# Hybrid decoder layer on one core: the up projection's issue order written by hand, its sums put back into PSUM, and some low parts moved from GpSimd to VectorE

## The chip, the cores and the metric

The kernel runs on one core of one Trainium2 chip. The metric is the device time of one execution in microseconds (us), the median of several runs. Engines are named as in the profile: PE is TensorE (its matmuls), PEld its weight loads, DVE VectorE, ACT ScalarE, POOL GpSimd, SP SyncE, which issues most DMAs here. A name such as L1346 is a line of the kernel before; lines of the changed kernel are given as such.

## What is computed

One decoder layer over 1024 tokens of 1024 channels: an attention mixer and a state-space mixer side by side, merged through `w_o`, normalised, and then a gated MLP with a causal depthwise convolution of width 3:

```python
mix = (sigmoid(g_a) * y_a + sigmoid(g_b) * y_b) @ w_o
x = layer_norm(alpha * x + gate1 * mix) * ln1_g + ln1_b

h2 = layer_norm(x) * (1.0 + scale2) + shift2
up = causal_depthwise_conv(h2 @ w_up, conv_w, conv_b)     # 1024 -> 2 * 2816
val, gte = split(up, 2, axis=-1)
ff = (silu(gte) * val) @ w_down                            # 2816 -> 1024
x = layer_norm(alpha * x + gate2 * ff) * ln2_g + ln2_b
```

The change touches the stretch from the rows of `w_o` to the end of the up projection, `h2 @ w_up` with convolution and gate.

## The kernel before

**Precision.** A float32 operand is split into a high part (copied by ACT into a narrower format, fp32r) and a low part (value minus high part). A product takes three matmuls: high by high, high by low, low by high (L1346 to L1348).

**Rows of `w_o`** (L1403 to L1442). Eight rows of 128 tokens. Each is 48 matmuls on PE, then a residual sum `hr` on DVE (L1420), two layer norms (DVE statistics, ACT scaling), and the store of `x1`. Rows 0 to 5 apply the first norm's gain on DVE and its bias on POOL (L1425, L1426), rows 6 and 7 with two DVE instructions (`ln_affine`). The rows are then transposed by PE in `h2_rows`, first rows 0 to 3 together, then 4 and 5, then 6 and 7. The first half of the output tiles is scaled by DVE (L1213), the second by ACT (L1215). Results are `y0` (tokens 0 to 511) and `y1` (512 to 1023).

**Up projection.** The output is worked through in 22 pairs `f`, each 128 value channels and the 128 gate channels that go with them. Instead of eight block products of half the inner dimension and half the tokens, a pair takes seven products (Strassen's scheme), numbered 1 to 7. Product `j` multiplies a combination of weight blocks, made anew for each pair, with a combination of `h2` blocks `ops[j]`, made once (3, 5, 6, 7 lie in tiles `h2a`, 1, 2, 4 in `h2b`). Each is 12 matmuls of 128x512 (4 inner chunks by 3). Products gather in four PSUM banks: `Z` (2, then 4 on top) and `Y` (5, then 3 on top) are the two halves of one two-bank tile `up`; `X` (1, then 7) and `V` (6) are tiles of their own (`upX`, `upV`). Tile's dependency tracking treats the two halves of `up` as one tile.

- Weight combinations of a pair: `plain` (products 2 and 5: ACT copy L1295, low part on POOL L1296), `less` (3 and 4: DVE subtractions L1306, ACT copy L1309, low part on DVE L1310), `cross` (1: DVE L1314, ACT L1315, POOL L1316), `sums` (6 and 7: DVE L1321, ACT L1322, POOL L1323).
- Sums between products: `t` takes a copy of product 2 by ACT (L1357), then adds product 5 on DVE (L1355); `r` is product 1 minus `t` on DVE (L1359). `t` and `r` are SBUF tiles that a profile names `bias` (in one pair `upt`).
- `finish` makes the four quarters of the pair: `Y` and `Z` are complete in PSUM, the other two are added up by DVE in an SBUF tile `u` (L1368 to L1371). Then comes the convolution for the gate (`e` = 1) and the value (`e` = 0): tap 0 on ACT (L1379), taps 1 and 2 on DVE (L1382), two narrow DVE instructions across the seam of the token halves (L1384), Silu on ACT (L1386), the product of gate and value on POOL (L1387) and the store of `ff_d`.

**Operands.** `set_operand` makes a part of `ops[j]`: the sum on one engine (L1196), the high part on ACT (L1198), the low part on `e1` (L1199). In `h2_sums` `e1` is DVE or POOL in turn.

**Order.** The whole program goes through Tile's scheduler, which simulates it and puts every engine's instructions in an order of its own choosing; the order of the code above is only a start. In the steady part PE's order in a step is 2, 6 and 5 of the pair, 1 of the next pair, then 4, 3 and 7. Engines execute in order; an instruction that waits holds up all behind it on its engine. The down projection (L1561 to L1574) follows; its first matmuls (`dn`) need low parts of `w_down` and of `ff`.

Of the kernel before, what the change touches and what calls it, by code (L numbers as in the profile page):

```python
# [33 lines left out]
def kernel(  # L34
# [1166 lines left out]
    def h2_rows(i0, ni, ys):  # L1201
        n = P * ni
        for q in range(4):
            p = ps(name="h2p")
            if ni == 4:
                p1 = ps(name="h2p")
            for e in range(2):
                k = q + 4 * e
                pe = (p, p1)[e] if ni == 4 else p[:, n * e:n * e + n]
                for i4 in range(ni):  # L1210
                    TE.transpose(pe[:, P * i4:P * i4 + P], h2s[i0 + i4][:, P * k:P * k + P], ident)
                if e == 0:
                    V.tensor_scalar(ys[q][e], pe, mod[:, 2, k:k + 1], mod[:, 3, k:k + 1], op0=OP.mult, op1=OP.add)  # L1213
                else:
                    A.activation(ys[q][e], pe, AF.Identity, bias=mod[:, 3, k:k + 1], scale=mod[:, 2, k:k + 1])  # L1215
# [63 lines left out]

    class Pair:  # L1280
        def __init__(self, f):
            self.f, self.w, self.bank, self.done, self.t = f, {}, {}, set(), None
# [5 lines left out]
        def plain(self, es):  # L1288
# [4 lines left out]
            for e in es:  # L1293
                src = self.c1[:, 4:8] if e else self.c0[:, 0:4]
                A.activation(h[:, e], src, AF.Copy)  # L1295
                G.tensor_sub(l[:, e], src, h[:, e].bitcast(F32))  # L1296
                w[5 if e else 2] = h[:, e], l[:, e]

        def less(self, es):
            w = self.w  # L1300
            if 0 in es:
                self.t34 = wtile("C", "uh"), wtile("C", "ul"), Bt([P, 2, 4, P], name="us")
            h, l, t = self.t34
            for e in es:
# [1 line left out]
                V.tensor_sub(t[:, e], src[:, 4 * e:4 * e + 4], src[:, 4 - 4 * e:8 - 4 * e])  # L1306
# [3 lines left out]
            V.tensor_sub(l[:, v], t[:, v], h[:, v].bitcast(F32))  # L1310

        def cross(self):
            t, t1 = wtile("C", "u1"), Bt([P, 4, P], name="us1")
            V.tensor_add(t1, self.c0[:, 0:4], self.c1[:, 4:8])  # L1314
            A.activation(t[:, 0], t1, AF.Copy)  # L1315
            G.tensor_sub(t[:, 1], t1, t[:, 0].bitcast(F32))  # L1316
            self.w[1] = t[:, 0], t[:, 1]

        def sums(self):
            h, l, t = wtile("wh", "uh"), wtile("wl", "ul"), Bt([P, 2, 4, P], name="us")  # L1320
            V.tensor_add(t.rearrange("p a k c -> p (a k) c"), self.c0, self.c1)  # L1321
# [1 line left out]
            G.tensor_sub(l, t, h.bitcast(F32))  # L1323
# [10 lines left out]
        def product(self, j, part=None):  # L1334
# [9 lines left out]
            for q in range(4):  # L1344
# [3 lines left out]
                TE.matmul(po, wl[:, q], h, start=False, stop=(q == 3), skip_group_check=True)  # L1348

            t, r = self.parts()  # L1350
            if j in (2, 5):
                if j == 2 and 5 in self.done:
                    V.tensor_add(t[:, c], po, t[:, c])
                elif j == 5 and 2 in self.done:
                    V.tensor_add(t, po, t)  # L1355
                else:
                    A.activation(t[:, c], po, AF.Copy)  # L1357
            elif j == 1:
                V.tensor_sub(r, po, t)  # L1359
            self.done.add(j)  # L1360

        def finish(self):
            bk = self.bank
            t, r = self.parts()
            lo, hi = slice(0, 512), slice(512, 1024)
            u = Bt([P, 1024], name="u")
            ug, uv = u[:, lo], u[:, hi]
            V.tensor_add(ug, bk["V"], r)  # L1368
            V.tensor_add(ug, ug, bk["Y"])  # L1369
            V.tensor_sub(uv, bk["X"], t)  # L1370
            V.tensor_add(uv, uv, bk["Z"])  # L1371
            cv = [Bt([P, 1024], name="cv") for _ in range(2)]

            for e, (a, b) in ((1, (bk["Y"], ug)), (0, (uv, bk["Z"]))):
                m = self.f + NF * e
                dst = cv[e]
                tap = lambda d: cw[:, 2 - d, m:m + 1]
                for half, src in ((lo, a), (hi, b)):
                    A.activation(dst[:, half], src, AF.Identity, bias=cw[:, 3, m:m + 1], scale=tap(0))  # L1379
                for d in (1, 2):  # L1380
                    for c0, src, n in ((d, a, 512 - d), (512 + d, b, 512 - d)):
                        V.scalar_tensor_tensor(dst[:, c0:c0 + n], src[:, 0:n], tap(d), dst[:, c0:c0 + n],  # L1382
                                               op0=OP.mult, op1=OP.add)
                    V.scalar_tensor_tensor(dst[:, 512:512 + d], a[:, 512 - d:512], tap(d), dst[:, 512:512 + d],  # L1384
                                           op0=OP.mult, op1=OP.add)
# [219 lines left out]
```

## Time and profile before

| | us |
|---|---|
| runs before | 1692.97, 1693.41, 1701.58 (median 1693.41) |
| the profiled execution | 1698.03 |
| its span, first to last instruction | 1696.3 |
| PE busy in the span | 1569.0 (92%) |
| DVE busy | 1239.6 (73%) |
| ACT busy | 691.1 (41%) |
| POOL busy | 706.2 (42%) |

Stages are cut by what PE works on: the rows of `w_o` end at 920 us, the up projection's first products and its fill-up run from there to about 1035 us, the steady pairs from 1035.3 to 1381.2 us, then come two last pairs and the down projection to the end. A timeline row gives start, duration, engine, line, operation, output<-inputs, and in brackets how long the engine was idle before it and on whom it waited. A group row gives the count, the summed and the mean time in ns. Matmuls overlap: what counts is the distance between two starts.

### The profile page before, as it was taken

How to read it: one execution, taken by the hardware profiler on the slowest of the kernel's cores; microseconds unless marked ns; L12 is line 12 of the kernel's file. 1: busy time of each engine (PE TensorE's matmuls, PEld its weight loads, DVE VectorE, ACT ScalarE, POOL GpSimd, SP SyncE). 2: the span in 40 equal slices, each digit the busy share in tenths (PEclk: the TensorE clock that was granted, in tenths of full speed). 3: DMA queues.
4: the chain of work that ended last, by engine and by line, in shares of the span. 5: the costliest groups of instructions: out<-in, count | busy, mean ns of one | idle time of the engine just before them, and what ended most of it. 6: DMA issues, size and time to landing. Idle time of an engine off the chain costs nothing.

```text
span 1696.3 us, 21512 instructions
## 1 busy us (share of the span) xinstructions
PE 1569.0 (92%) x7707; PEld 1304.0 (77%) x7707; DVE 1239.6 (73%) x2263; ACT 691.1 (41%) x1303; POOL 706.2 (42%) x584
## 2 busy tenths in 40 slices
PE   6987899999999999999998579999999998899996
PEld 4976787878989999788787357777777776688885
DVE  8699766565399999553658876888888888855448
ACT  4423223224399999421323433444344333311101
POOL 4342355400066566222536634544444555521105
PEclk8998999999999999999999789999999999999998
DMA  9235544622200010443411112222222227522102
GB/s 341 70 113 151 167 146 152 202 64 79 71 20 1 14 38 2 145 132 123 137 62 63 38 50 87 75 75 75 75 75 75 75 88 251 208 100 99 39 2 99
DMA packets 150128, 164.36 MB, mean 97 GB/s; under 512 B 20633, under 2 KB 123777, under 8 KB 150021
## 3 DMA queue, kind: packets, MB, share of 16 engines
q1 hardware_dynamic: 146357, 151.74, 27.9%
q10 hardware_dynamic: 3664, 11.24, 1.7%
q8 instruction: 61, 1.00, 0.2%
q14 instruction: 46, 0.38, 0.1%
HBM read 132.04 MB, written 30.91 MB: 96 GB/s over the span
## 4 chain that ended last, share of the span: by engine, by line
PE 57%; DVE 27%; issue 6%; ACT 5%; POOL 2%; DMA 2%; SPq 0%; DVEq 0%; ACTq 0%; POOLq 0%
DVE cv L1382 5%; PE dn L1472 4%; PE dn L1474 4%; PE dn L1473 4%; PE oacc L1008 3%; PE pT L1019 3%; PE up L1346 3%; PE up L1348 2%; PE up L1347 2%; DVE us L1321 2%; PE zm L128 2%; PE zm L130 2%; ACT cv L1379 2%; PE zm L129 2%; DVE us L1306 2%
## 5 line engine op out<-in xcount | busy, mean ns | idle before, releaser
L982 POOL TENSOR_SCALAR Pm<-Pm,gate,fc 128x64 f32<-128x64 f32 (+4 forms) x192 | 123.8, 659 | 57.3 <-DVE fc L980 56.8
L1472 PE MATMUL dn<-dnh,fh 128*128 128x512 f32 x320 | 124.9, 390 | 4.5 <-DVE facc L1570 4.5
L1296 POOL TENSOR_TENSOR ul<-wr,uh 128x512 fp32r<-128x512 f32 x44 | 77.7, 1785 | 115.4 <-ACT uh L1295 115.4
L1474 PE MATMUL dn<-dnh,fl 128*128 128x512 f32 x320 | 124.1, 389 | 1.6 <-DVE fl L1463 1.6
L1570 DVE SCALAR_TENSOR_TENSOR facc<-facc,dn 128x512 f32<-128x512 f32 x96 | 64.7, 681 | 83.3 <-PE dn L1474 83.3
L1473 PE MATMUL dn<-dnl,fh 128*128 128x512 f32 x320 | 124.5, 389 | 0.0
L978 ACT ACTIVATE Pm<-Pm,ng 128x64 f32<-128x64 f32 (+6 forms) x192 | 114.7, 602 | 6.5 <-DVE ng L959 5.0
L130 PE MATMUL zm<-hTh,wl 128*128 128x512 f32 x256 | 101.8, 398 | 13.1 <-DVE wl L113 13.1
L112 ACT ACTIVATE wh<-wr 128x1024 fp32r<-128x1024 f32 (+3 forms) x59 | 57.7, 978 | 137.8 <-PE ya L129 30.6
L111 POOL TENSOR_TENSOR wr<-wr,g2b 128x1024 f32<-128x1024 f32 x22 | 63.3, 2885 | 120.5 <-DMA wr<-in_w_down_dram 79.4
L1023 DVE TENSOR_TENSOR Pt<-pT,Pt 128x512 fp32r<-128x512 f32 (+1 forms) x160 | 100.6, 642 | 9.7 <-ACT Pt L1022 8.7
L128 PE MATMUL zm<-hTh,wh 128*128 128x512 f32 x256 | 101.9, 398 | 2.9 <-ACT wh L112 2.5
L1008 PE MATMUL oacc<-Pt,Vs 128*128 128x256 f32 x528 | 102.6, 304 | 0.9 <-DVE Pt L1023 0.4
L129 PE MATMUL zm<-hTl,wh 128*128 128x512 f32 x256 | 101.2, 395 | 0.0
L113 DVE TENSOR_TENSOR wl<-wr,wh 128x1024 fp32r<-128x1024 f32 (+2 forms) x40 | 51.8, 1294 | 64.4 <-ACT wh L112 64.2
L1019 PE MATMUL pT<-ident,Pm 128*128 128x128 f32 x592 | 91.3, 273 | 1.9 <-DVE yl L1082 1.0
L1379 ACT ACTIVATE cv<-u,cw 128x512 f32<-128x512 f32 x44 | 35.6, 809 | 140.3 <-DVE u L1369 132.7
L1022 ACT ACTIVATE Pt<-pT 128x512 fp32r<-128x512 f32 (+1 forms) x160 | 87.4, 560 | 13.1 <-PE pT L1019 12.1
L1382 DVE SCALAR_TENSOR_TENSOR cv<-u,cw,cv 128x511 f32<-128x511 f32 x88 | 74.8, 851 | 19.7 <-ACT cv L1379 18.8
L1347 PE MATMUL up<-h2b,uh 128*128 128x512 f32 (+1 forms) x184 | 72.2, 393 | 15.1 <-POOL h2b L1199 15.1
L1346 PE MATMUL up<-h2b,uh 128*128 128x512 f32 (+1 forms) x184 | 74.4, 406 | 12.1 <-DVE bias L1355 9.0
L1323 POOL TENSOR_TENSOR ul<-us,uh 128x1024 fp32r<-128x1024 f32 x22 | 52.8, 2398 | 74.8 <-ACT uh L1322 71.2
(507 smaller groups left out, 4871.0 us busy)
## 6 DMA issues: line engine op xcount, KB each, us to landing
wr<-in_w_up_dram SPq DMA_DIRECT2D x44, 512.0 KB, 3.8
wr<-in_w_in_dram SPq DMA_DIRECT2D x32, 512.0 KB, 4.2
wr<-in_w_ada_dram SPq DMA_DIRECT2D x32, 512.0 KB, 4.1
ff_d<-cv SPq DMA_DIRECT2D x22, 512.0 KB, 2.8
wr<-in_w_down_dram SPq DMA_DIRECT2D x22, 512.0 KB, 4.0
fl<-ff_d SPq DMA_DIRECT2D x22, 512.0 KB, 6.0
ar<-in_w_ada_dram SPq DMA_DIRECT2D x16, 512.0 KB, 9.4
zm_d<-sg ACTq DMA_DIRECT2D x16, 512.0 KB, 2.9
```

Of the source, the lines that this page charges most:

```text
L128: TE.matmul(po, wh, rh, start=start, stop=False, skip_group_check=skip)
L129: TE.matmul(po, wh, rl, start=False, stop=False, skip_group_check=skip)
L130: TE.matmul(po, wl, rh, start=False, stop=stop, skip_group_check=skip)
L978: A.activation(Pm[ii][:, c0:c0 + n], Pm[ii][:, c0:c0 + n], AF.Exp, bias=ng[:, ii, br:br + 1], scale=-1.0, accum_out=dn[:, ii, br:br + 1])
L982: G.tensor_scalar(Pm[ii][:, c0:c0 + n], Pm[ii][:, c0:c0 + n], gate[:, i, 3 * h + br:3 * h + br + 1], fc[:, ii, br:br + 1], op0=OP.mult, op ...
L1008: TE.matmul(acc[:, a0:a0 + 256], vt, ptile[:, hl, 256 * w:256 * w + 256], start=(first and n == 1), stop=(last and n == nmm), skip_group_c ...
L1019: TE.transpose(p[:, o:o + P], Pm[e][:, c0:c0 + P], ident)
L1346: TE.matmul(po, wh[:, q], h, start=(q == 0 and j not in (3, 4, 7)), stop=False, skip_group_check=True)
L1382: V.scalar_tensor_tensor(dst[:, c0:c0 + n], src[:, 0:n], tap(d), dst[:, c0:c0 + n], op0=OP.mult, op1=OP.add)
L1472: TE.matmul(p, ff[0][:, c0], wd[0][:, s], start=(e == 0), stop=False)
L1473: TE.matmul(p, ff[0][:, c0], wd[1][:, s], start=False, stop=False)
L1474: TE.matmul(p, ff[1][:, c0], wd[0][:, s], start=False, stop=(e == len(fs) - 1))
```

## The change

- `h2_rows`: all scaling of transposed tiles is done by ACT. `h2_sums`: all low parts are done by DVE. All eight rows use `ln_affine`. `h2_first` is called after row 4 instead of 5, `h2_next(0)` after row 6 instead of after the rows.
- `Pair`: the low parts of `plain`, `cross` and `sums` go to DVE for pairs 0 and 1 (`self.e`), to POOL for the others. The methods are cut into an add, a high and a low step, so that they can be put at different places. `less`'s low tile moves to another SBUF pool.
- `finish` becomes `value_hi`, `value_lo`, `gate_sum`, `gate` and `out`. The tile `u` is gone: the value's first half is added up in bank `X`, the gate's second half in bank `V`, both by DVE instructions that write PSUM, and ACT and DVE take all taps from PSUM.
- The reading of products 1, 2 and 5 becomes `take(j)`, which in pairs from 2 on is called where the step puts it.
- Pairs 1 to 21 run in `step(f)`, inside `tc.manual_schedule`, which keeps DVE, ACT, POOL and PE in the order of the code. PE's order is 2, 5, 1, 4, 7, 6, 3. What follows the last pair (loading `g2b`, which scales `w_down`, then `ff` and `x1`) now stands behind the loop.

```diff
@@ h2_rows
-                if e == 0:
-                    V.tensor_scalar(ys[q][e], pe, mod[:, 2, k:k + 1], mod[:, 3, k:k + 1], op0=OP.mult, op1=OP.add)
-                else:
-                    A.activation(ys[q][e], pe, AF.Identity, bias=mod[:, 3, k:k + 1], scale=mod[:, 2, k:k + 1])
+                A.activation(ys[q][e], pe, AF.Identity, bias=mod[:, 3, k:k + 1], scale=mod[:, 2, k:k + 1])
@@ h2_sums
-            e0, e1 = (V, (V if q % 2 else G)) if c1 - c0 < 512 else (V, (V if q else G))
-            set_operand(j, q, a, b, op, e0, e1, c0, c1, a if j != 2 else None)
+            set_operand(j, q, a, b, op, V, V, c0, c1, a if j != 2 else None)
@@ class Pair
+            self.e = V if f < 2 else G
...
-                G.tensor_sub(l[:, e], src, h[:, e].bitcast(F32))
+                self.e.tensor_sub(l[:, e], src, f32(h[:, e]))
...
+        def take(self, j, c=slice(0, 512)):
             t, r = self.parts()
+            po = self.bank["Z" if j == 2 else "Y" if j == 5 else "X"][:, c]
+            if j == 1:
                 V.tensor_sub(r, po, t)
+            elif 7 - j in self.done:
+                V.tensor_add(t[:, c], po, t[:, c])
+            else:
+                A.activation(t[:, c], po, AF.Copy)
...
+        def value_hi(self):
+            t, _ = self.parts()
+            Z = self.bank["Z"]
+            self.tap0(0, hi, Z)
+            V.tensor_sub(t, Z, t)
+            self.taps(0, hi, Z)
+        def value_lo(self):
+            t, _ = self.parts()
+            X = self.bank["X"]
+            V.tensor_add(X, X, t)
+            self.tap0(0, lo, X)
+            self.taps(0, lo, X)
+            self.seam(0, X)
+        def gate_sum(self):
+            _, r = self.parts()
+            V.tensor_add(r, self.bank["V"], r)
+        def gate(self):
+            _, r = self.parts()
+            Y, g = self.bank["Y"], self.bank["V"]
+            V.tensor_add(g, Y, r)
+            self.tap0(1, lo, Y)
+            self.tap0(1, hi, g)
+            self.taps(1, lo, Y)
+            self.taps(1, hi, g)
+            self.seam(1, Y)
@@ rows of w_o
-        hr = (Ct if i < 4 else Bt)([P, 1024], name="hr")
+        hr = (Ct if i < 6 else Bt)([P, 1024], name="hr")
-        if i >= 6:
-            ln_affine(xi, hr, l1g, l1b)
-        else:
-            normalize(xi, hr)
-            V.tensor_mul(xi, xi, l1g)
-            G.tensor_add(xi, xi, l1b)
+        ln_affine(xi, hr, l1g, l1b)
@@ the loop over pairs
+    def step(f):
+        pr, last = pairs[f], pairs.pop(f - 1)
...
+        two = product(2)
+        last.gate()
+        if two:
+            pr.take(2)
+        last.out()
+        five = product(5)
+        if nx:
+            nx.cross_add()
+            nx.less_sub((0, 1))
+            nx.cross_hl()
+            nx.less_hi((0, 1))
+        if five:
+            pr.take(5)
+        if nx:
+            nx.plain((1, 0))
+            nx.sums_add()
+        product(1)
+        if f > 1:
+            pr.take(1)
+        if nx:
+            nx.less_lo((0, 1))
+        product(4)
+        pr.value_hi()
+        product(7)
+        pr.value_lo()
+        product(6)
+        pr.gate_sum()
+        if nx:
+            nx.sums_hl()
+        product(3)
+    with tc.manual_schedule(engines={V.engine, A.engine, G.engine, TE.engine}):
+        for f in range(1, NF):
+            step(f)
```

**VectorE in a steady step.** Of the kernel before, from the first gate sum on (`u` is the SBUF tile, `bias` is `t` or `r`, `wr` the raw weights, `us` their combinations):

```order
L1368 TENSOR_TENSOR u<-upV,bias 128x512
L1369 TENSOR_TENSOR u<-u,up 128x512
L1382 SCALAR_TENSOR_TENSOR cv<-u,cw,cv 128x511
L1382 SCALAR_TENSOR_TENSOR cv<-u,cw,cv 128x510
L1370 TENSOR_TENSOR u<-upX,bias 128x512
L1371 TENSOR_TENSOR u<-u,up 128x512
L1314 TENSOR_TENSOR us_10416<-wr 128x512
L1306 TENSOR_TENSOR us<-wr 128x512 x2
L1321 TENSOR_TENSOR us<-wr 128x1024
```

Of the changed kernel, from the gate's sum of the pair before on:

```order
L1431 TENSOR_TENSOR upV<-up,bias 128x512
L1400 SCALAR_TENSOR_TENSOR cv<-up,cw,cv 128x511
L1400 SCALAR_TENSOR_TENSOR cv<-up,cw,cv 128x510
L1400 SCALAR_TENSOR_TENSOR cv<-upV,cw,cv 128x511
L1400 SCALAR_TENSOR_TENSOR cv<-upV,cw,cv 128x510
L1406 SCALAR_TENSOR_TENSOR cv<-up,cw,cv 128x1
L1406 SCALAR_TENSOR_TENSOR cv<-up,cw,cv 128x2
L1333 TENSOR_TENSOR us_10033<-wr 128x512
L1311 TENSOR_TENSOR us<-wr 128x512 x2
L1387 TENSOR_TENSOR bias<-up,bias 128x512
L1344 TENSOR_TENSOR us<-wr 128x1024
L1385 TENSOR_TENSOR bias<-upX,bias 128x512
```

The gate's taps now come all at once and read PSUM; the weight combinations follow in one piece with the take of product 5 (L1387) in between, the wide one (L1344) behind it, and then the take of product 1 (L1385).

**ScalarE in a steady step.** Before, the copy of product 2 (L1357) with what stands around it:

```order
L1379 ACTIVATE cv<-up,cw 128x512
L1379 ACTIVATE cv<-u,cw 128x512
L1357 ACTIVATE bias<-up 128x512
L1315 ACTIVATE u_10271<-us_10272 128x512
L1309 ACTIVATE uh<-us 128x1024
```

In the changed kernel the copy is L1389, behind the gate's two first taps (L1395) and ahead of Silu (L1440):

```order
L1395 ACTIVATE cv<-up,cw 128x512
L1395 ACTIVATE cv<-upV,cw 128x512
L1389 ACTIVATE bias<-up 128x512
L1440 ACTIVATE cv<-cv 128x1024
L1337 ACTIVATE u_10183<-us_10176 128x512
L1315 ACTIVATE uh<-us 128x1024
```

On PE product 5, which follows product 2 directly now, writes the other half of the tile that this copy reads; before, product 6 stood between them.

**GpSimd from the last operand in `h2a` to the steady part.** Before (`h2b`, `h2a` are low parts of operands, `ul` and `u_...` those of weights):

```order
L1199 TENSOR_TENSOR h2a<-h2s,h2a 128x512
L1296 TENSOR_TENSOR ul<-wr,uh 128x512
L1199 TENSOR_TENSOR h2b<-bias,h2b 128x256 x2
L1199 TENSOR_TENSOR h2b<-h2y,h2b 128x256 x3
L1199 TENSOR_TENSOR h2b<-bias,h2b 128x256
L1199 TENSOR_TENSOR h2b<-h2y,h2b 128x256
L1199 TENSOR_TENSOR h2a<-h2y,h2a 128x512 x2
L1199 TENSOR_TENSOR h2b<-bias,h2b 128x256
```

In the changed kernel, where L1441 is the product of gate and value of pair 0:

```order
L1199 TENSOR_TENSOR h2a<-h2y,h2a 128x512 x4
L1441 TENSOR_TENSOR cv<-cv 128x1024
L1338 TENSOR_TENSOR u_9064<-us_9057,u_9064 128x512
L1302 TENSOR_TENSOR ul<-wr,uh 128x512 x2
L1350 TENSOR_TENSOR ul<-us,uh 128x1024
```

All that stood between them on POOL (the low parts of operands 1, 2, 4, 6, 7 and of the weights of pairs 0 and 1) stands in VectorE's queue now.

More of the change, by code (lines that the diff above doesn't have):

```diff
@@ L1312, in cross @@
[L1312 to L1316, printed above, removed]
[L1317 to L1321 removed]
+            A.activation(self.t34[0][:, v], self.us[:, v], AF.Copy)
@@ new lines, in less_lo, with less, cross_add @@
+        def less_lo(self, es):
+            h, l = self.t34
+            v = slice(None) if len(es) == 2 else es[0]
+            V.tensor_sub(l[:, v], self.us[:, v], f32(h[:, v]))
+            for e in es:
+                self.w[3 + e] = h[:, e], l[:, e]
+            if 1 in es:
+                self.us = None
+        def less(self, es):
+            self.less_sub(es)
+            self.less_hi(es)
+            self.less_lo(es)
+        def cross_add(self):
+            self.us1 = sp.tile([P, 4, P], F32, name="us1", tag="misc", bufs=2)
+            V.tensor_add(self.us1, self.c0[:, 0:4], self.c1[:, 4:8])
@@ L1360, in product @@
[L1360 to L1385, printed above, removed]
@@ new lines, in taps, with seam @@
+        def taps(self, e, half, src):
+            m, dst, c = self.f + NF * e, self.cv[e], half.start
+            for d in (1, 2):
+                V.scalar_tensor_tensor(dst[:, c + d:c + 512], src[:, 0:512 - d], cw[:, 2 - d, m:m + 1],
+                                       dst[:, c + d:c + 512], op0=OP.mult, op1=OP.add)
+        def seam(self, e, src):
+            m, dst = self.f + NF * e, self.cv[e]
+            for d in (1, 2):
+                V.scalar_tensor_tensor(dst[:, 512:512 + d], src[:, 512 - d:512], cw[:, 2 - d, m:m + 1],
+                                       dst[:, 512:512 + d], op0=OP.mult, op1=OP.add)
@@ L1429 @@
         h2s[i] = hr
-        if i == 5:
+        if i == 4:
             h2_first()
@@ L1508 @@
         pairs[0].product(j, 1)
-    pairs[0].cross()
-    pairs[0].sums()
+    pairs[0].cross_add()
+    pairs[0].cross_hl()
+    pairs[0].sums_add()
+    pairs[0].sums_hl()
     h2_sums(6)
@@ L1514 @@
     pairs[1].less((1,))
-    for j in (2, 4):
-        pairs[1].product(j)
+    pairs[1].product(2)
     pairs[0].product(6)
     h2_sums(1)
+    pairs[1].product(4)
     pairs[0].product(1)
@@ L1522, with product @@
     y0 = y1 = None
-    pairs[1].cross()
-    pairs[1].sums()
-    for f in range(NF):
-        pr = pairs[f]
-        for j in (2, 5):
+    pairs[0].value_hi()
+    pairs[0].value_lo()
+    pairs[0].gate_sum()
+    pairs[1].cross_add()
+    pairs[1].cross_hl()
+    pairs[1].sums_add()
+    pairs[1].sums_hl()
+    def step(f):
+        pr, last = pairs[f], pairs.pop(f - 1)
+        nx = None
+        if f < NF - 1:
+            nx = pairs[f + 1] = Pair(f + 1)
+            nx.low()
+        def product(j):
@@ L1528 @@
             if j in pr.w:
                 pr.product(j)
-        if f:
-            pairs.pop(f - 1).finish()
-        for j in (1, 4, 6, 3, 7):
-            if j in pr.w:
-                pr.product(j)
-        if 0 < f < NF - 1:
-            nx = pairs[f + 1] = Pair(f + 1)
-            nx.low()
-            nx.plain((0, 1))
-            nx.cross()
-            nx.less((0, 1))
-            nx.sums()
-        if f == NF - 2:
-            g2b = Bt([P, 1024], name="g2b")
-            brow(g2b, gr_d, D)
-            W.scales[1] = g2b
@@ L1546 @@
[L1546 to L1555 removed]
+                return True
+        two = product(2)
@@ new lines, in step @@
+        product(7)
[8 more added lines that the diff above has]
+            step(f)
+    pr = pairs.pop(NF - 1)
+    ops.clear()
+    g2b = Bt([P, 1024], name="g2b")
+    brow(g2b, gr_d, D)
+    W.scales[1] = g2b
+    load_ff(len(DG[0]))
+    for f_ in DG[0]:
+        prep_down(f_)
+    facc = [Ct([P, 1024], name="facc") if i % 4 < 2 else
+            sp.tile([P, 1024], F32, name="facc", tag=("wh", "wl")[i % 2], bufs=2) for i in range(NT)]
@@ L1556 @@
+    for i in range(NT):
+        SP.dma_start(facc[i], ap(x1_d, i * P * D, [D, P], [1, D]))
+    pr.gate()
+    pr.out()
     snaps = None
```

65 lines of the change are left out of this document (34 added, 31 removed).

## The prediction

> **What bounds the kernel now.** I read the clock, then the chain of waits, then busy times by stage.
>
> ```profile
> core 0: 1696.3 us, clock 0.969
> PE 57%; DVE 27%; issue 6%; ACT 5%; POOL 2%; DMA 2%; SPq 0%; DVEq 0%; ACTq 0%; POOLq 0%
> 825.00:920.00 95.00, 93.07 (x420) 76.56 (x419) 61.87 (x130) 35.66 (x57) 58.45 (x37) 0.98 0.27 95
> 920.00:1025.00 105.00, 70.38 (x275) 52.38 (x273) 84.95 (x148) 40.05 (x72) 47.74 (x24) 0.80 0.15 45
> 1035.30:1381.20 345.90, 333.64 (x1428) 265.06 (x1428) 281.26 (x392) 141.14 (x187) 169.83 (x85) 1.00 0.24 76
> ```
>
> The stage rows give start:end, length, then busy PE, PEld, DVE, ACT, POOL, granted clock, DMA share and GB/s. Among the stages that the change touches, PE bounds the rows of `w_o` (93.07 of 95 us) and nearly bounds the steady pairs (333.64 of 345.9). The fill-up is different: PE worked 70.38 of 105 us, at a clock of 0.80. So there are two places to gain, little per step in the steady part and much at once in the fill-up.
>
> **The steady step.** The period and its two stalls:
>
> ```profile
> 1075.99 0.69 DVE L1369 TENSOR_TENSOR u<-u,up 128x512 f32<-128x512 f32 x1 [2.58 <-PE up L1348]
> 1096.32 0.69 DVE L1369 TENSOR_TENSOR u<-u,up 128x512 f32<-128x512 f32 x1 [2.58 <-PE up L1348]
> 1078.51 0.39 PE L1346 MATMUL up<-h2b,uh 128*128 128x512 f32 x1
> 1081.23 0.39 PE L1346 MATMUL upV<-h2a,uh 128*128 128x512 f32 x1
> 1082.13 0.50 PE L1348 MATMUL upV<-h2a,ul 128*128 128x512 f32 x1 [0.28 <-POOL ul L1323]
> 1090.55 0.50 PE L1346 MATMUL up<-h2b,uh 128*128 128x512 f32 x1 [0.42 <-DVE bias L1355]
> ```
>
> A step takes 1096.32 - 1075.99 = 20.33 us. An undisturbed product takes 1081.23 - 1078.51 = 2.72, seven take 19.04. The missing 1.29 are the two bracketed waits. Both go: product 6 now comes sixth, long after its low part, and product 4 comes two products after 5, so the take of 5 (L1355 before) has 2.7 us of cover.
>
> In their place comes one wait. Product 5 follows 2 at once, and the copy of 2 by ACT must read its half of the tile first. Before, 6 stood between. The fill-up of before has this very sequence once:
>
> ```profile
> 1024.53 0.39 PE L1348 MATMUL up<-h2b,ul 128*128 128x512 f32 x1
> 1025.61 0.50 PE L1346 MATMUL up<-h2a,uh 128*128 128x512 f32 x1 [0.69 <-ACT bias L1357]
> 1025.94 0.40 PE L1347 MATMUL up<-h2a,uh 128*128 128x512 f32 x1
> 1028.23 0.39 PE L1348 MATMUL up<-h2a,ul 128*128 128x512 f32 x1
> ```
>
> From last to first matmul 1.08 instead of 2.72 / 12 = 0.227, so 0.85 more; and the product took 1028.23 + 0.23 - 1025.61 = 2.85, 0.13 more. Price 0.98 a step. New step 19.04 + 0.98 = 20.02, **0.31 less than now**. Behind the waiting product all of PE queues; ahead of the copy on ACT stand only the gate's two first taps.
>
> **Does VectorE keep up?** Per step, from these groups:
>
> ```profile
> L1321 DVE TENSOR_TENSOR us<-wr 128x1024 f32<-128x1024 f32 x17 | 39.4, 2315 | 0.0
> L1314 DVE TENSOR_TENSOR us<-wr 128x512 f32<-128x512 f32 x17 | 37.8, 2222 | 0.0
> L1306 DVE TENSOR_TENSOR us<-wr 128x512 f32<-128x512 f32 x34 | 21.8, 678 | 0.0
> L1382 DVE SCALAR_TENSOR_TENSOR cv<-up,cw,cv 128x511 f32<-128x511 f32 x34 | 25.3, 743 | 3.2 <-ACT cv L1379 3.2
> L1382 DVE SCALAR_TENSOR_TENSOR cv<-u,cw,cv 128x511 f32<-128x511 f32 x34 | 25.2, 742 | 16.1 <-ACT cv L1379 16.1
> L1355 DVE TENSOR_TENSOR bias<-up,bias 128x512 f32<-128x512 f32 x17 | 11.6, 680 | 0.0
> L1310 DVE TENSOR_TENSOR ul<-us,uh 128x1024 fp32r<-128x1024 f32 x17 | 20.7, 1218 | 0.0
> L1296 POOL TENSOR_TENSOR ul<-wr,uh 128x512 fp32r<-128x512 f32 x34 | 61.9, 1841 | 96.4 <-ACT uh L1295 96.4
> L1316 POOL TENSOR_TENSOR u<-us,u 128x512 fp32r<-128x512 f32 x17 | 27.5, 1616 | 22.0 <-ACT u L1315 22.0
> L1387 POOL TENSOR_TENSOR cv<-cv 128x1024 f32<-128x1024 f32 x17 | 40.7, 2394 | 0.0
> ```
>
> DVE was busy 281.26 of 345.9 us, 16.5 of 20.33 a step. The change keeps the counts: four quarter sums or differences, eight taps, four seams. A tap costs the same from PSUM (743) as from SBUF (742). L1314 took 2222 ns against 678 for L1306, which has the same shape: 1.5 us of waiting for POOL, and L1321 about 1.1 by the same reasoning (2315 against 1218 for L1310). DVE instructions with one input in PSUM (680, 743) show nothing of that.
>
> No DVE write into PSUM of this shape is in the trace. From both sides: 0.1 less than 0.68 (no result goes to SBUF), or double; I take 0.68, the nearest row. Of two such writes a step, that into `V` holds up the gate's second tap and so the copy of product 2. Even doubled (+0.7) it delays nothing: I place it at 0.2 to 0.9 after product 2 began, the two ACT taps then end at 2.5, and product 2 ends at 2.9. The other end, a gain, isn't used by anybody.
>
> The chain that matters on DVE in a step, counted from product 2's start with the rows above (0.60 to 0.68 for a 512 sum, 0.66 to 0.74 a tap): gate sum to 0.9, taps and seams 1.8 to 5.2, `cross` and `less` 5.1 to 7.0, take of 5 to 7.6 (product 4 asks for it at 9.1). POOL's product of gate and value follows Silu, asks at 6.4, gets the port at 7.0, runs 2.4 to 9.4. Then DVE's wide `sums` add to 10.5 and the take of 1 to 11.1; product 7 asks for it at 11.9. So **0.8 us of slack**, and some 1.3 us over the whole step.
>
> [...]
>
> **The fill-up.** PE's two largest waits there, what was behind the first, and the rows for the count below:
>
> ```profile
> 964.99 0.58 PE L1347 MATMUL up<-h2b,uh 128*128 128x256 f32 x1 [13.36 <-POOL h2b L1199]
> 1016.00 0.80 PE L1346 MATMUL upX<-h2b,u 128*128 128x512 f32 x1 [4.06 <-ACT u L1315]
> 950.21 14.05 POOL L1199 TENSOR_TENSOR h2b<-h2y,h2b 128x256 fp32r<-128x256 f32 x1 [5.29 <-ACT h2b L1198]
> 956.31 0.41 DVE L1199 TENSOR_TENSOR h2b<-h2y,h2b 128x256 fp32r<-128x256 f32 x1
> 992.36 0.69 DVE L1359 TENSOR_TENSOR bias<-upX,bias 128x512 f32<-128x512 f32 x1 [11.17 <-PE upX L1348]
> 999.64 0.39 PE L1348 MATMUL upX<-h2a,ul 128*128 128x512 f32 x1
> L1215 ACT ACTIVATE h2y<-h2p,mod 128x256 f32<-128x256 f32 x8 | 4.1, 563 | 1.7 <-PE h2p L1211 1.7
> ```
>
> A 0.41 us instruction took 14.05 us on POOL, since DVE ran sums of two SBUF inputs without a pause, and PE lost 13.36 us at one spot. The change puts these low parts on DVE. They don't become free: about 6 of 128x256 (0.34 apart) and 4 of 128x512 (0.60) move from POOL into DVE's queue ahead of the last products of pairs 0 and 1, plus the weights' low parts, 4 + 2 + 1 us. But DVE was idle there (11.17 us before 992.36).
>
> By hand through the new order: row 7's norm is ready 3 us earlier, since the POOL work that DVE waited for in the rows is gone; the second part of operands 2 and 4 is complete at about 961.5 instead of 965, though ACT has 8 more scalings of 0.56 (L1215); low parts of operand 1 about 972. Pairs 0 and 1 then end on PE at about 990, against 999.64 + 0.4 = 1000 now: 10 us. New on the other side: pair 0's gate, Silu and product come after that in the written order, POOL reaches pair 2's low parts only at about 1001, and PE idles 11 us and restarts at half clock (the matmul at 1016.00, after such a pause, took 0.80 instead of 0.39). By my count pair 2 ends at 1023.5. Before, that point is 1035.3, where the steady part starts: **11.5 us** gained. This is the softest number: if ACT or DVE is late by a few us in each of three waits, it shrinks to 0; if pair 0's gate slips in beside the products, up to 20.
>
> In the `w_o` rows the moves change nothing (PE 93.07 of 95).
>
> **The end.** Pairs 20 and 21, and the first down products:
>
> ```profile
> 1381.14 0.69 DVE L1369 TENSOR_TENSOR u<-u,up 128x512 f32<-128x512 f32 x1 [2.58 <-PE up L1348]
> 1404.44 0.69 DVE L1369 TENSOR_TENSOR u<-u,up 128x512 f32<-128x512 f32 x1 [4.19 <-PE up L1348]
> 1417.41 0.61 PE L1472 MATMUL dn<-bh,fh 128*128 128x512 f32 x2
> 1430.85 0.39 PE L1474 MATMUL dn<-bh,fl 128*128 128x512 f32 x1
> 1434.19 0.50 PE L1472 MATMUL dn<-bh,fh 128*128 128x512 f32 x1 [2.95 <-DVE u L1370]
> L111 POOL TENSOR_TENSOR wr<-wr,g2b 128x1024 f32<-128x1024 f32 x22 | 63.3, 2885 | 120.5 <-DMA wr<-in_w_down_dram 79.4
> ```
>
> Pair 20 took 1404.44 - 1381.14 = 23.3 us, since POOL's scaling of `w_down` got in; in the new order that follows pair 21: 3.3 gained. From 1404.44 to 1434.19 are 29.75 us, in which PE did pair 21 and 18 early down matmuls (the first two and the last are shown; 18 x 0.227 = 4.1) and stood for 3: without the early ones 25.65. New: 20.0, and then a wait for the first down operands, all of whose preparation now follows the loop. What is late next is the scaling of `w_down` on POOL, 2.9 us apiece. I take a wait of 4, so 25.65 - 24 = 1.65 gained; bounds are no wait at all (-5.65) and three scalings in a row after 3 us (12, +6.3).
>
> **Sum.** Fill-up -11.5 (0 to -20), 17 steady steps x -0.31 = -5.3, pair 20 -3.3, pair 21 with the wait -1.65 (-5.65 to +6.3): -21.8. Against the profiled execution's own 1698.03 that is 1676.2. It stands 4.6 above the median of the runs, 1693.41, so the median comes to **1671.6**, -1.3%.
>
> **Rivals.**
>
> - *The fill-up gives nothing.* ACT has all the scalings besides all high parts, 40 us busy of 105 before, and each group of operands is released by it. If its lateness eats the 11.5, the sum is -10.3: 1683. For it speaks that PE waited for ACT there too (1016.00); against it the 14.05 us row. 0.17.
> - *The copy doesn't hold up product 5.* Then a step is 19.04 and the sum is 18 x 0.98 = 17.6 lower: 1654. Against it speaks the row at 1025.61 with this very wait. 0.07.
> - *Slower: POOL keeps the port.* If after the product of gate and value POOL's three low parts run on without letting DVE in (2.4 + 1.6 + 3.6 us), the wide `sums` add starts at 14.6 instead of 9.4, the take of 1 ends at 16.3, and product 7 is 4.4 late in every step. At half clock after such a pause, another 2: 18 x 6.4 = +115, 1787. It decides from 0.8 us on, DVE's slack. Of a smaller form, the second `less` subtraction waits behind the product of gate and value: take of 5 at 10.0 instead of 9.1, 18 x 1.1 = +20, 1692. Against both: POOL's 14.05 us shows DVE keeping the port while its instructions follow each other, and L1310 stood at 1218 though POOL's `plain` low parts ran around it. 0.06 and 0.08.
> - *The end costs.* The wait for `w_down` is 12 us or more: 1680 and up. For it speaks L111's 2.9 us apiece. 0.10.
>
> **How the numbers follow.** Forecast 1671.6, chance 0.52, with its own range 1661 to 1681. The range 1651 to 1693 leaves out the first form of the slower rival and tails on both sides. About 0.5% (8.5 us, between 1685 and 1702) is what a measurement of this kernel can tell from no change. Faster: the forecast, the second rival, most of the end's and two thirds of the first: 0.74. Same: the rest of these and the smaller form of POOL's: 0.16. Slower: 0.10.
>
> **What would show it.** Steady period 20.0 with one wait, on ACT's copy (changed line L1389), of about 0.7 idle, and none on DVE; the wide `sums` add (L1344) near 2 us, ending before product 7; no POOL operand low part in the fill-up, PE's gap there under 8 us, pair 2 complete near 1024; some 11 us of idle PE ahead of pair 2's first low part; first down matmul about 4 us after pair 21. I am wrong if PE waits for DVE's take of 1 (L1385) in the steady part, or if the fill-up ends at 1035 again.

## The result

| | before | changed |
|---|---|---|
| median of the runs, us | 1695.29 | 1677.04 |
| lowest and highest, us | 1692.97, 1701.58 | 1673.91, 1680.39 |
| profiled execution, us | 1698.03 | 1675.66 |
| ratio changed / before | | 0.9878, 95% interval 0.9850 to 0.9905 |

The changed kernel is 1.2% faster; the forecast was 1671.6 against 1693.41 (the median of the three runs on record by then), a ratio of 0.987.

### The profile after

Of the changed kernel: clock, chain of waits, and busy times (start:end, length, then PE, PEld, DVE, ACT, POOL, granted clock, DMA share, GB/s) for the `w_o` rows, the fill-up, and 16 steady steps:

```profile
core 0: 1673.9 us, clock 0.975
PE 73%; DVE 16%; ACT 5%; issue 4%; DMA 2%; POOL 0%; SPq 0%; DVEq 0%; ACTq 0%; POOLq 0%
825.00:920.00 95.00, 93.02 (x426) 76.00 (x425) 72.85 (x131) 31.09 (x54) 43.68 (x29) 1.00 0.25 89
920.00:1022.40 102.40, 74.42 (x310) 57.01 (x309) 88.00 (x167) 49.81 (x87) 19.85 (x10) 0.87 0.21 67
1042.38:1362.69 320.31, 309.32 (x1345) 251.08 (x1344) 263.84 (x368) 133.46 (x176) 175.23 (x81) 1.00 0.25 79
```

DVE's share of the chain fell from 27% to 16%. POOL works 19.85 us in the fill-up instead of 47.74, and the granted clock there is 0.87 instead of 0.80.

The steady step, as PE's and DVE's timelines show it (start, duration, engine, line, operation, idle before and on whom):

```profile
1104.73 0.39 PE L1375 MATMUL up<-h2b,ul 128*128 128x512 f32 x1
1105.80 0.50 PE L1373 MATMUL up<-h2a,uh 128*128 128x512 f32 x1 [0.69 <-ACT bias L1389]
1114.10 0.39 PE L1373 MATMUL upX<-h2a,uh 128*128 128x512 f32 x1
1125.82 0.50 PE L1373 MATMUL up<-h2a,uh 128*128 128x512 f32 x1 [0.69 <-ACT bias L1389]
...
1102.44 0.70 DVE L1431 TENSOR_TENSOR upV<-up,bias 128x512 f32<-128x512 f32 x1 [1.25 <-PE up L1375]
1109.73 2.85 DVE L1344 TENSOR_TENSOR us<-wr 128x1024 f32<-128x1024 f32 x1
1112.50 0.68 DVE L1385 TENSOR_TENSOR bias<-upX,bias 128x512 f32<-128x512 f32 x1
```

The period is 1125.82 - 1105.80 = 20.02, with one wait, product 5 for the copy of 2. The sum written to PSUM took 0.70. The take of product 1 ended at 1113.18 and product 7 started at 1114.10: 0.92 us of slack.

Where the profiled executions part (22.37 us in all), by the start of the gate's sum (L1369 before, L1431 after) in pairs 2, 19 and 20:

| | before, us | changed, us | difference | forecast |
|---|---|---|---|---|
| until the steady part (pair 2's sum) | 1035.34 | 1022.36 | -12.98 | -11.5 |
| 17 steps to pair 19's sum | 345.80 | 340.33 | -5.47 | -5.3 |
| pair 20 | 23.30 | 20.03 | -3.27 | -3.3 |
| pair 21 and all behind it | 293.59 | 292.94 | -0.65 | -1.65 |

### The profile page after: what moved, and what is told of

Same layout as the page of the kernel before. It is cut to its first block, busy times and chain, and to the rows that moved or that the text cites. A ratio compares the mean times of both kernels' runs of the same rounds, so it can differ in the third digit from the quotient of the medians.

```text
span 1673.9 us, 21550 instructions
## 1 busy us (share of the span) xinstructions
PE 1556.6 (93%) x7707; PEld 1302.2 (78%) x7707; DVE 1246.5 (74%) x2270; ACT 692.6 (41%) x1309; POOL 672.2 (40%) x559
## 4 chain that ended last, share of the span: by engine, by line
PE 73%; DVE 16%; ACT 5%; issue 4%; DMA 2%; POOL 0%; SPq 0%; DVEq 0%; ACTq 0%; POOLq 0%
PE up L1373 5%; PE up L1375 4%; PE up L1374 4%; PE dn L1522 4%; PE dn L1521 4%; PE dn L1523 4%; PE oacc L1008 3%; PE zm L130 2%; PE zm L128 2%; PE zm L129 2%; PE pT L1019 2%; PE upX L1374 2%; PE upX L1375 2%; PE upX L1373 2%; ACT Pm L978 2%
## 5 line engine op out<-in xcount | busy, mean ns | idle before, releaser
L1441 POOL TENSOR_TENSOR cv<-cv 128x1024 f32<-128x1024 f32 x22 | 62.0, 2816 | 190.2 <-ACT cv L1440 110.0
L111 POOL TENSOR_TENSOR wr<-wr,g2b 128x1024 f32<-128x1024 f32 x22 | 62.4, 2848 | 123.0 <-DMA wr<-in_w_down_dram 110.6
L1373 PE MATMUL up<-h2a,uh 128*128 128x512 f32 x176 | 71.8, 408 | 17.1 <-ACT bias L1389 14.4
L1395 ACT ACTIVATE cv<-up,cw 128x512 f32<-128x512 f32 x44 | 34.3, 779 | 120.6 <-PE up L1375 63.8
L1400 DVE SCALAR_TENSOR_TENSOR cv<-up,cw,cv 128x511 f32<-128x511 f32 x88 | 65.7, 747 | 19.8 <-ACT cv L1395 18.3
L1008 PEld LDWEIGHTS oacc<-Pt,Vs 128*128 128x128 f32 x528 | 75.5, 190 | 5.4 <-DVE Pt L1023 3.1
L113 POOL TENSOR_TENSOR wl<-wr,wh 128x1024 fp32r<-128x1024 f32 (+1 forms) x19 | 37.9, 1992 | 99.4 <-ACT wh L112 88.0
```

The lines of the kernel that those rows point to most:

```text
L1008: TE.matmul(acc[:, a0:a0 + 256], vt, ptile[:, hl, 256 * w:256 * w + 256], start=(first and n == 1), stop=(last and n == nmm), skip_group_c ...
L1373: TE.matmul(po, wh[:, q], h, start=(q == 0 and j not in (3, 4, 7)), stop=False, skip_group_check=True)
```

## The experiments

Each ratio below is to the kernel before, measured on the same chip. The start of the steady part varies between profiles: end_early, whose order up to there is that of the changed kernel, has pair 2's sum at 1026.04 instead of 1022.36. So 4 us in the fill-up of one profile say nothing by themselves.

### Does the copy hold the step, and how near is the port?

**six_second.** Product 6 between 2 and 5.

```diff
         last.out()
+        product(6)
         five = product(5)
...
         pr.value_hi()
+        pr.gate_sum()
         product(7)
         pr.value_lo()
-        product(6)
-        pr.gate_sum()
```

> The changed kernel with product 6 issued second (2, 6, 5, 1, 4, 7, 3), so that ACT's copy of product 2 has 2.72 us of cover; gate_sum moved ahead of product 7. Theory (the copy is all that keeps PE from its floor): steady period 19.04 to 19.2 instead of 20.02, no wait on L1389; 20 steps x 0.9 give 18 to 20 us, about 1657. Rival (VectorE and GpSimd have no room below 20 us): the period stays above 19.5, with PE waiting for the value's taps (L1400) ahead of product 3 or for the low part of sums on POOL ahead of product 6; 1666 or more.

1673.26 us, ratio 0.9848 (0.9819 to 0.9876); period 19.66. PE in this kernel:

```profile
1120.10 0.50 PE L1373 MATMUL up<-h2a,uh 128*128 128x512 f32 x1 [0.32 <-DVE cv L1400]
1139.76 0.50 PE L1373 MATMUL up<-h2a,uh 128*128 128x512 f32 x1 [0.32 <-DVE cv L1400]
```

The wait on the copy is gone and the step is 0.36 shorter, so the copy did hold it. But the rival's wait stands in its place: product 3 writes the tile whose other half the value's taps still read, and between 4 and 3 only product 7 is left as cover. 20 x 0.36 = 7.2 us were won in the loop; the medians differ by 4, and in the profiles the steady part starts 3.3 later (pair 2's sum at 1025.64).

**probe_dve.** One more VectorE sum of two SBUF inputs ahead of the take of product 1; its result isn't used.

```diff
             nx.sums_add()
+            xt = Bt([P, 512], name="xt")
+            V.tensor_add(xt, *pr.parts())
         product(1)
```

> The changed kernel with one more VectorE sum (two SBUF inputs, 128x512, 0.68 us by itself; its result isn't used) between the wide sums add and the take of product 1, whose slack is 0.9 us in the profile. Rival that the port changes hands between instructions: the probe waits for GpSimd's low part (1.6 us), the take ends about 1 us after product 7's turn, steady period near 21.1 and about 20 us more. Theory that VectorE keeps the port as long as its instructions follow each other: the probe takes 0.6, the take ends within its slack, the period stays at 20.02 and the time within 2 us.

1700.4 us, ratio 1.0013 (0.9998 to 1.0028); period 21.17. DVE, POOL and PE in this kernel:

```profile
1118.91 2.83 DVE L1344 TENSOR_TENSOR us<-wr 128x1024 f32<-128x1024 f32 x1
1120.63 2.27 POOL L1338 TENSOR_TENSOR u<-us,u 128x512 fp32r<-128x512 f32 x1
1121.67 1.77 DVE L1610 TENSOR_TENSOR xt<-bias 128x512 f32<-128x512 f32 x1
1123.55 0.69 DVE L1385 TENSOR_TENSOR bias<-upX,bias 128x512 f32<-128x512 f32 x1
1124.29 0.50 PE L1373 MATMUL upX<-h2a,uh 128*128 128x512 f32 x1 [0.84 <-DVE bias L1385]
```

A 0.68 us sum took 1.77, product 7 waited, and one such instruction a step cost 23 us, more than the change had won. POOL's L1338, 1.29 us long in sched, took 2.27 here: it started at 1120.63, during the wide add, and ended at 1122.90, 1.16 after the add; the next VectorE sum ended 0.54 after it. So the wait that the forecast's slower rival needs is seen in this kernel, and the take of product 1 is 0.9 us away from it. The rival's own form, three low parts of POOL in a row without letting VectorE in, isn't seen: here the two engines took turns, one instruction each.

"The port" is a name for this waiting of the two engines on each other, which the rows show where VectorE's instruction has two SBUF inputs. In the kernel before, L1314 took 2.23 us where L1306, of the same shape, took 0.68, and ended 0.56 after POOL's L1323:

```profile
1079.67 2.40 POOL L1323 TENSOR_TENSOR ul<-us,uh 128x1024 fp32r<-128x1024 f32 x1 [3.35 <-ACT uh L1322]
1080.40 2.23 DVE L1314 TENSOR_TENSOR us<-wr 128x512 f32<-128x512 f32 x1
```

**pe_by_hand.** Only PE keeps the written order.

```diff
-    with tc.manual_schedule(engines={V.engine, A.engine, G.engine, TE.engine}):
+    with tc.manual_schedule(engines={TE.engine}):
```

> The changed kernel with PE alone in the written order (2, 5, 1, 4, 7, 6, 3); DVE, ACT and POOL go to the scheduler. It tells whether the order of products or that of the other engines holds the changed kernel at 20.02 us a step where the scheduler reaches 19.04. Theory (the order of products: 5 directly behind 2): the wait for ACT's copy stays, period 20.0, 1672 to 1680. Rival (the other engines' order): period under 19.5, 1665 or less.

1686.51 us, ratio 0.9932 (0.9909 to 0.9954); period 20.4 to 20.7.

```profile
1108.32 0.59 ACT L1389 ACTIVATE bias<-up 128x512 f32<-128x512 f32 x1
1108.97 0.51 PE L1373 MATMUL up<-h2a,uh 128*128 128x512 f32 x1 [0.98 <-ACT bias L1389]
```

The wait on the copy stays, as the theory said, but it is longer, and the time is above the 1672 to 1680 that were expected: the scheduler put a 1.05 us copy of weights (L1315) ahead of it on ACT. So the other three engines' written order is better for this order of products than the scheduler's.

**sched.** All of it to the scheduler; the instructions are the same.

```diff
-    with tc.manual_schedule(engines={V.engine, A.engine, G.engine, TE.engine}):
+    if True:
```

> The changed kernel with pairs 1 to 21 given to the scheduler instead of the written order (the same instructions, PSUM sums included). Theory (the steady gain is that of the order): period 20.3 or more, with other waits than ACT's copy, 6 us or more slower than the changed kernel. Rival (the gain comes from the PSUM sums and the split of the methods): period at or under 20.0, within 3 us.

1651.85 us, ratio 0.9732 (0.9706 to 0.9758): the rival, and far beyond it. Of this kernel 16 steps by the windows view, then three rows of DVE and ACT:

```profile
1043.23:1347.71 304.48, 304.48 (x1345) 252.17 (x1344) 225.78 (x370) 133.56 (x176) 153.50 (x80) 1.00 0.26 83
...
1102.00 1.22 DVE L1344 TENSOR_TENSOR us<-wr 128x1024 f32<-128x1024 f32 x1
1105.05 1.25 DVE L1320 TENSOR_TENSOR ul<-us,uh 128x1024 fp32r<-128x1024 f32 x1
1116.51 0.60 ACT L1389 ACTIVATE bias<-up 128x512 f32<-128x512 f32 x1 [1.01 <-PE up L1375]
```

PE is busy throughout, 304.48 of 304.48 us, 19.03 a step. PE's order there is 5, 6, 1, 4, 7, 2 of the next pair, 3 (the first two matmuls of 6 ahead of 5). Pulling 2 of the next pair ahead of 3 gives the copy 3 as cover, the take of 5 products 6 and 1, and the value's taps 7 and 2. The wide sum of weights (L1344) comes early on DVE, while POOL is idle (1098.11 to 1103.91), and takes 1.22 instead of 2.85; their low part (L1320) takes 1.25 instead of 1.71, though POOL is at work then (L1302, 1103.91 to 1107.45). DVE is busy 225.78 / 16 = 14.1 us a step against 263.84 / 16 = 16.5 in the written order. The fill-up is no better than that of the changed kernel (pair 2's sum at 1023.95). That the written order of PE keeps the step from 19.04 even when the other engines go to the scheduler, pe_by_hand shows; how much the DVE order adds wasn't taken apart.

**sched_sbuf and sums_sbuf.** Both PSUM sums back in an SBUF tile, under the scheduler and in the written order.

```diff
-            V.tensor_add(X, X, t)
+            u, X0 = Bt([P, 512], name="u"), X
+            X = u
+            V.tensor_add(X, X0, t)
...
-            Y, g = self.bank["Y"], self.bank["V"]
+            Y, g = self.bank["Y"], Bt([P, 512], name="u")
```

> The version under the scheduler with the gate's and the value's sums in an SBUF tile instead of PSUM. Theory (the two sums cost the same in either place, and the tile is no bottleneck): the period stays at 19.0 to 19.1, within 4 us of 1652. Rival (PSUM sums are what lets the scheduler reach PE's floor): period 19.5 or more, 1660 or more.

> The changed kernel in its written order with both sums in an SBUF tile instead of PSUM. Theory (a DVE sum written to PSUM costs 0.68 to 0.70, as one written to SBUF): period 20.02, within 3 us of the changed kernel. Rival (the write into PSUM holds up what follows): the gate's chain shortens by 0.1 us or more and the time changes by 4 us or more.

In the written order: period 20.02 as expected, the sum 0.69 instead of 0.70; 1683.89 us, ratio 0.9919 (0.9893 to 0.9946), so 7 us above the changed kernel, outside what was expected. In the profiles 5.5 of them lie ahead of the steady part, which starts at 1027.88, PE having stood 12.13 us ahead of pair 1's product 7 instead of 8.86. DVE's order there is another one too: a sum and a low part of weights (L1344 and L1350, 1.21 and 1.22 us), which in the changed kernel run at 974.96 and 977.32, stand at 987.83 and 990.48 between the instructions of pair 0's gate. So these 7 us aren't shown to be the price of an SBUF tile. Under the scheduler: 1691.49 us, ratio 0.9971 (0.9957 to 0.9985), period 20.62. In that kernel:

```profile
1105.25 2.66 DVE L1406 SCALAR_TENSOR_TENSOR cv<-u,cw,cv 128x1 f32<-128x1 f32 x2
1105.49 2.40 POOL L1350 TENSOR_TENSOR ul<-us,uh 128x1024 fp32r<-128x1024 f32 x1 [2.71 <-ACT uh L1349]
1117.11 0.50 PE L1373 MATMUL up<-h2b,uh 128*128 128x512 f32 x1 [1.29 <-DVE bias L1387]
```

Two seams over one and two columns, with both inputs in SBUF (`u` and `cv`), took 2.66 us beside POOL's L1350 and ended with it, at 1107.91 and 1107.89. Two from PSUM take 0.46 in the changed kernel, and one from PSUM beside POOL's L1302 (1113.67 to 1117.58) took 0.20 in this one, at 1116.98. And PE waits for the take of 5, for which the scheduler chose an order with too little cover. The runs don't tell how much is the port and how much the other order that the scheduler found. What is shown: under the scheduler the version with the PSUM sums, and the order found for it, is 40 us faster; in the written order the period is the same with both.

### The fill-up

**lows_alone.** The kernel before with the low parts alone moved to DVE.

```diff
-            e0, e1 = (V, (V if q % 2 else G)) if c1 - c0 < 512 else (V, (V if q else G))
+            e0, e1 = V, V
...
-                G.tensor_sub(l[:, e], src, h[:, e].bitcast(F32))
+                (V if self.f < 2 else G).tensor_sub(l[:, e], src, h[:, e].bitcast(F32))
```

(and likewise in `cross` and `sums`)

> The kernel before with this one part of the change: all low parts of h2_sums and those of pairs 0 and 1 on DVE, everything else in the scheduler's order. Theory: the wait of 13.36 us for a starved POOL instruction goes, and 8 to 12 us with it: ratio to before 0.993 to 0.995. Rival (it helps only together with the order written by hand, since DVE becomes as late as POOL was): ratio 0.998 to 1.002.

1683.67 us, ratio 0.9928 (0.9906 to 0.9950), as the theory said. PE's three longest waits between 945 and 960 are now 4.21, 2.82 and 1.73 us, all for DVE's L1199; the kernel before waits 13.36 for POOL's, at 964.99:

```profile
949.74 0.58 PE L1347 MATMUL up<-h2b,uh 128*128 128x256 f32 x1 [4.21 <-DVE h2b L1199]
```

The steady part starts at 1018.52, 16.8 us earlier, 3.8 more than in the whole change (within what profiles differ by). The period is 20.34, as before. By the medians this part alone wins 12 of the change's 18 us.

**lows_back.** The changed kernel with this part undone.

```diff
-            set_operand(j, q, a, b, op, V, V, c0, c1, a if j != 2 else None)
+            e1 = (V if q % 2 else G) if c1 - c0 < 512 else (V if q else G)
+            set_operand(j, q, a, b, op, V, e1, c0, c1, a if j != 2 else None)
...
-            self.e = V if f < 2 else G
+            self.e = G
```

> The changed kernel with the low parts of h2_sums again on DVE and POOL in turn and those of pairs 0 and 1 on POOL. Theory (the gain of the fill-up, 13 us, comes from taking these off POOL): a low part on POOL is starved again, the steady part starts 8 to 13 us later, 1685 to 1690. Rival (the fill-up gains by the row norms, the earlier h2_next or the written order): within 3 us of the changed kernel.

1685.64 us, ratio 0.9943 (0.9920 to 0.9965); steady part from 1030.30. The starved instruction is back, and PE waits for it by way of ACT:

```profile
963.68 9.75 POOL L1199 TENSOR_TENSOR h2b<-h2y,h2b 128x512 fp32r<-128x512 f32 x1 [3.23 <-ACT h2b L1198]
973.47 0.63 ACT L1198 ACTIVATE h2b<-h2y 128x512 fp32r<-128x512 f32 x1 [6.24 <-POOL h2b L1199]
975.09 0.80 PE L1374 MATMUL upV<-h2a,uh 128*128 128x512 f32 x1 [5.95 <-ACT uh L1350]
```

The high part behind it on ACT waits 6.24 us, and the weights' copy that PE needs (L1350) stands behind that. An earlier wait of PE, for DVE's L1199, is 7.75 us instead of 2.85.

**rows_back.** The changed kernel with the norms of rows 0 to 5 as before.

```diff
-        ln_affine(xi, hr, l1g, l1b)
+        if i >= 6:
+            ln_affine(xi, hr, l1g, l1b)
+        else:
+            normalize(xi, hr)
+            V.tensor_mul(xi, xi, l1g)
+            G.tensor_add(xi, xi, l1b)
```

> The changed kernel with the norms of rows 0 to 5 as before (ACT, then gain on DVE and bias on POOL). Theory (PE bounds the rows, so their norms matter only where row 7 waits behind them): 0 to 3 us slower than the changed kernel. Rival (the earlier operands of the fill-up come from here): 6 us or more slower.

1685.11 us, ratio 0.9927 (0.9901 to 0.9953): the rival; steady part from 1031.70. Of this kernel, DVE's wait in row 5's norm and PE's waits ahead of the transposes, then those of PE in the changed one:

```profile
924.76 1.29 DVE L240 BATCH_NORM_STATS2 bn<-xi 128x6 f32<-128x512 f32 x2 [2.29 <-POOL xi L1480]
931.17 3.19 PE L1211 MATMUL h2p<-ident,hr 128*128 128x128 f32 x12 [5.75 <-ACT hr L1269]
939.63 1.11 PE L1211 MATMUL h2p<-ident,hr 128*128 128x128 f32 x4 [5.27 <-ACT hr L1269]
```

```profile
927.75 2.05 PE L1211 MATMUL h2p<-ident,hr 128*128 128x128 f32 x8 [3.72 <-ACT h2y L1212]
930.61 1.84 PE L1211 MATMUL h2p<-ident,hr 128*128 128x128 f32 x4 [0.80 <-ACT h2y L1212]
```

PE bounds the rows themselves (93.02 of 95 us in the changed kernel), but the transposes behind them wait: at 931.17 for row 5, whose norm went the long way over ACT, DVE and POOL, and at 939.63 for row 6, whose norm came behind that one on DVE and behind the scaling of rows 4 and 5 on ACT.

The three parts don't add up: lows_alone reaches the steady part at 1018.52, the whole change at 1022.36, and without the low parts or without the row norms it is 1030.30 or 1031.70.

### The end

**end_early and six_end.** `g2b` loaded at the last step but one and the first down operands prepared in the last step, by itself and with six_second's edit; the same lines behind the loop go.

```diff
+        if f == NF - 2:
+            g2b = Bt([P, 1024], name="g2b")
+            brow(g2b, gr_d, D)
+            W.scales[1] = g2b
         two = product(2)
...
+        if f == NF - 1:
+            load_ff(len(DG[0]))
+            for f_ in DG[0]:
+                prep_down(f_)
```

> The changed kernel with g2b loaded at the last step but one and the first two down operands prepared in the last step, where POOL is idle for 8 us. Theory (the end costs because the scaling of w_down starts only after the loop and then collides with DVE's low parts): PE's gaps between pair 21 and 1440, 15 us in the changed kernel, fall by 5 to 7 us: about 1670. Rival (the loads of ff and the later groups are what is late): the first gaps go, but they come back before 1440; within 2 us of 1676.

> Both of the edits above. If they are independent, their gains add: 23 to 27 us below the changed kernel, 1650 to 1653. If the end is bound by the loads, only the first gain is left, about 1657.

end_early: 1672.88 us, ratio 0.9848 (0.9819 to 0.9876). The changed kernel had these waits, and reached the second group of down products at 1440.64:

```profile
1403.10 0.96 PE L1521 MATMUL dn<-bh,fh 128*128 128x512 f32 x3 [0.40 <-ACT bh L112]
1406.39 0.50 PE L1522 MATMUL dn<-bl,fh 128*128 128x512 f32 x1 [2.34 <-DVE bl L113]
1411.46 0.50 PE L1522 MATMUL dn<-bl,fh 128*128 128x512 f32 x1 [2.70 <-DVE bl L113]
```

end_early reached it at 1437.75, though its steady part had started 3.7 us later: 6.6 us won between, within what was expected. six_end: 1673.82 us, ratio 0.9863 (0.9846 to 0.9879), not additive and far from the 1650 to 1653 of independent gains. There POOL's low part for product 6 of pair 21 came behind the early scaling of `w_down`:

```profile
1384.71 0.50 PE L1375 MATMUL upV<-h2a,ul 128*128 128x512 f32 x1 [1.81 <-POOL ul L1350]
```

And a wait of 2.79 us for a low part of `w_down`, which end_early had removed, is back.

**sched_end.** The same edit under the scheduler.

> The version under the scheduler (label sched, 1651.85 us, steady period 19.04) with g2b loaded at the last step but one and the first down operands prepared in the last step. From pair 21's end to the second group of down products PE there lost 9.5 us (31.3 us for 96 matmuls of 0.227). Theory (the scaling of w_down starts too late): 4 to 6 us less, about 1647. Rival (the loads of ff and of w_down set it): within 2 us of 1652.

1649.57 us, ratio 0.9715 (0.9692 to 0.9739), the fastest version of the study; 2.3 us below sched, with intervals that overlap, so its gain over sched isn't settled.

## Why the prediction was right

- **The sum.** The two profiled executions differ by 22.37 us, near the 21.8 of the forecast, but the medians by 18.25: the profiled execution before lies 2.74 above its median, the changed one 1.38 below. So 1671.6 was 5.4 too low. All four terms came out within 1.5 us, closer than two profiles of one order agree (3.7 in the fill-up), so that is partly luck.
- **The steady step** came out as worked out: 20.02 with the copy's wait, at the price read from the one place before where 5 followed 2. six_second shows the cause, by taking the wait away.
- **VectorE's slack** was put at 0.8 and was 0.92. The wide `sums` add, which waits for POOL's product of gate and value (that ended at 1111.49, the add at 1112.58), ended 10.3 after product 2's start where my sum had 10.5 (its row says 2.85 us, where I named 2 as the sign). probe_dve shows that one more sum there, with its wait for POOL, is longer than the slack. One argument against that rival was too strong: I took from the 14.05 us row (VectorE's sums stood there without idle from 949.55 to 963.68, POOL's low part ended at 964.26) that VectorE keeps the port while its instructions follow each other; in probe_dve GpSimd got in between two of them. Why it was starved for 14 us in one place and served at once in the other, the runs don't show.
- **PSUM operands.** The sum written to PSUM took 0.70 (0.69 to an SBUF tile in sums_sbuf; I had taken 0.68) and a tap from PSUM 0.747 in the mean, so neither price moved the sum. What the prediction didn't count is that a tap moved to PSUM gains freedom from waits: in the kernel before, the 88 taps from the SBUF tile (L1382) took 0.730 to 2.754 us (the longest at 1406.06, beside POOL's L111 and L1323), the 88 from PSUM 0.732 to 0.751; in the changed kernel all 176, from PSUM, took 0.733 to 0.752.
- **The fill-up** was right in size (13.0 for 11.5; end_early, with the same order, has 9.3; my two dates, 1035.3 and 1023.5, are 11.8 apart) and half wrong in its steps. The low parts' part is shown from both sides: the starved POOL instruction goes in lows_alone and returns in lows_back. "In the `w_o` rows the moves change nothing" fell: rows_back is 8 us slower, through the transposes. And the pause that I put ahead of pair 2's low part on POOL stands elsewhere, in PE's row of the changed kernel:

```profile
993.35 0.77 PE L1373 MATMUL upX<-h2a,uh 128*128 128x512 f32 x1 [8.86 <-DVE cv L1406]
992.52 0.69 DVE L1385 TENSOR_TENSOR bias<-upX,upt 128x512 f32<-128x512 f32 x1
```

  Product 7 of pair 1 waits for its take of product 1 (L1385), which the written order has behind pair 0's gate and pair 2's weights on DVE. The bracket names a seam that ended at about the same time; the same wait in sums_sbuf is put down to L1385 itself. A pause of 9 us instead of 11, at another place, left the sum nearly the same: that was luck.
- **The end** was mis-sized by 1 us, no more than profiles differ by: the first down matmul came 0.6 us after pair 21 instead of 4, but two waits of 2.3 and 2.7 for its low parts followed. DVE made them beside POOL's scalings, and the first took 2.66 us where a later one took 1.21:

```profile
1399.55 9.05 POOL L111 TENSOR_TENSOR wr<-wr,g2b 128x1024 f32<-128x1024 f32 x3 [8.23 <-DMA fl<-ff_d]
1403.68 2.66 DVE L113 TENSOR_TENSOR bl<-wr,bh 128x1024 fp32r<-128x1024 f32 x1
1410.20 1.21 DVE L113 TENSOR_TENSOR bl<-wr,bh 128x1024 fp32r<-128x1024 f32 x1
```

  end_early shows the place.
- **The rival of a lower floor** (product 5 not held up, 1654) was wrong for this order, but its time was within reach: sched has no wait at all in the step.

## What to carry to other kernels

Look at what stands between a product and the instruction that must read its bank before the next write: the price of a swap in an order is read from the one place of the old trace where the two already stand together. An order written by hand is worth comparing with the scheduler's on the same, reworked instructions; here the hand order cost 25 us (1677.04 against 1651.85), and under the scheduler the sums in PSUM were needed for the gain (1691.49 without them). Put instructions with two SBUF inputs where GpSimd is idle (1.22 us for the wide sum instead of 2.85), and give the others a PSUM input (taps took up to 2.75 us from SBUF in the kernel before, up to 0.75 from PSUM).
